# A hybrid retention / linear attention / window attention block: another place and order for the moving sums at both entries of the block products, and an earlier second weight pair

## The chip, the cores and the metric

The kernel runs on one core of one Trainium2 chip. The metric is device time in microseconds of one launch, the median of three runs. A core has TensorE (PE in the profile; PEld are its weight loads), VectorE (DVE), ScalarE (ACT), GpSimd (POOL) and SyncE (SP), which here only issues loads.

## The reference

One transformer block in fp32 on 1024 tokens of width 1024. What the change touches are two sets of large products: the input projection `h @ w_in`, and gate and up of the feed-forward part.

```python
h = rmsnorm(x, norm_mix_pre[l])
proj = h @ w_in[l]                      # q, k, gates of three branches, ...
...
x = x + rmsnorm(merged @ w_out[l], norm_mix_post[l])
h = rmsnorm(x, norm_ffn_pre[l])
f = (jax.nn.silu(h @ ffn_w_gate[l]) * (h @ ffn_w_up[l])) @ ffn_w_down[l]
x = x + rmsnorm(f, norm_ffn_post[l])
```

## The kernel before, in words

Each fp32 operand is kept as two halves, a rounded copy `hi` and the residual `lo`. `split` makes them: ScalarE casts `hi` (L127), then VectorE subtracts to get `lo` (L128; both lines are a helper's). A product of two such operands is three matmuls of 128x128 by 128x512 (L409, L410, L411): hi by hi, hi by lo, lo by hi.

The class `Pairs` (L362) computes two blocks of 128 output features (a *pair*, for instance one block of gate and one of up) over all 1024 tokens. It is a Winograd form of Strassen's scheme: the stationary side are the pair's weights, cut into a11, a12 (first raw tile), a21, a22 (second raw tile); the moving side are the activations, cut into four blocks B11, B12, B21, B22 by feature half and token half. Seven block products replace eight. Each block product is 12 matmuls for one pair:

- `p1` = a11 by b11 into bank x, copied out by `snap` (L359, tile sn); `p2` = a12 by b21 into bank y; the output x copy + y is made by `out` (L1255, L1256: VectorE addition, then Silu on ScalarE);
- `p6` = s2 by t2, on top of x; `p5` = s1 by t1 into bank z; `p7` = s3 by t3 on top of x; `p4` = a22 by t4 on top of x; `p3` = s4 by b22 on top of z.

The weight sums s1 to s4 of a pair are made by `sums` (L384, L386, L388, L389) and `split`; the weights a11 and a12 are split by `blocks` (L379: one cast of 128x1024 into wh and one residual into wl). The moving sums are made once for all pairs, by the class `Sums`: t3 = B22 - B12 (L560), t2 = t3 + B11 (L561), t1 = B22 - t2 (L573, written over t2), t4 = B21 - t2 (L572, in place). Each has four tiles (k = 0 to 3), and each tile is split into a pair of halves.

In the steady state of `steps` a pair's seven products follow one another and everything else runs beside them. At the *entry* the moving sums don't exist yet, so `lead` pairs are taken together: two at the first entry (input projection, `inp`, activations `hf`, from about 82 us), three at the second (`up`, activations `h2f`, from about 1524 us). The entry does all p1 and p2 first, holds back the additions of p2 (`held`), then s2 by t2 for all the lead pairs, then s1 by t1, s3 by t3, then p1 of the next pair (`nxt`), then a22 by t4, p2 of `nxt`, s4 by b22.

The second entry overlaps the end of the output projection. There, a loop over token tiles t (L1276) runs `out_mm(t)` on TensorE and `out_norm(t)` on ScalarE, VectorE and GpSimd; one to three turns later `out_transpose(t)` brings the token tile into `h2f`. The sums t2, t3 need `h2f` of all eight token tiles. `up.fetch` issues weight loads on SP's queue; `up.blocks` and `up.sums` split them.

The order of instructions in each engine's queue is written at build time by Tile's scheduler, which goes by the order in the source, by an estimate of when operands are ready, and by when a slot of a tile pool comes free. Two calls bind it: `keep_in_program_order` (the `Ordered` wrappers, on in part of the first entry) and `issue_after(ins)`, which puts the instructions of a block behind `ins` on its engine. On the chip each queue then runs in that order. The pools are `d` (45 tiles of 128x1024 fp32, or a hi/lo pair of 128x512), `b` (18 tiles of 128x512) and eight banks of PSUM.

Of the kernel before, what the change touches and what calls it, by code (L numbers as in the profile page):

```python
# [12 lines left out]
ALU = mybir.AluOpType  # L13
# [7 lines left out]
NK = D // P  # L21
# [58 lines left out]
def block_kernel(ctx: ExitStack, tc: tile.TileContext, x, vecs, rows, alpha2, w_in, w_branch,  # L80
                 w_out, w_gate, w_up, w_down, cst_in, out):
    nc = tc.nc
    pe, ve, se, po = (Ordered(tc, e) for e in (nc.tensor, nc.vector, nc.scalar, nc.gpsimd))
# [15 lines left out]
    def bt(n, dt=F32):  # L99
        return bp.tile([P, TH], dt, name=f"{n}_{nid()}", tag="b")  # L100
# [4 lines left out]
    def dt_(n, dt=F32):  # L105
        return dp.tile([P, 1024], dt, name=f"{n}_{nid()}", tag="d")

    def bpair(n):
        t = dt_(n, F32R)
        return t[:, :TH], t[:, TH:]  # L110
# [3 lines left out]
    def bank(n):  # L114
        return psp.tile([P, TH], F32, name=f"{n}_{nid()}", tag="ps")
# [10 lines left out]
    def split(hi, lo, src, eng=None):  # L126
        se.copy(out=hi, in_=src)  # L127
        return (eng or ve).tensor_tensor(out=lo, in0=src, in1=hi, op=ALU.subtract)  # L128
# [212 lines left out]
    KH = NK // 2  # L341
# [10 lines left out]
    def moving(name, src):  # L352
        pr = bpair(name)
        split(*pr, src)
        return pr

    def snap(ps):
        c = bt("sn")
        se.copy(out=c, in_=ps)  # L359
        return c  # L360

    class Pairs:  # L362
# [87 lines left out]
        def steps(self):  # L450
            keys, lead = self.keys, self.lead
            first = keys[:lead]
            x, z = self.x, self.z
            self.fetch(lead)
            held = []
            for i, n in enumerate(first):
                if n not in self.ops:
                    self.blocks(n)
                self.p1(n)
                yield  # L460
                held.append(self.p2(n, True))
                yield
            for n in first:
                if "s2" not in self.ops[n]:
                    self.sums(n)
            self.make("t2")
            self.products(first, [x[n] for n in first], "s2", "t2", False)
            for h in held:
                with tc.issue_after(self.sums_of.last.ins):
                    h()  # L470
            for n in first:
                self.sn[n].append(snap(x[n]))
            yield
            self.fetch(lead + 1)
            self.make("t1")
            for n in first:
                self.split(n, "s1")
                z[n] = bank("z")
            self.products(first, [z[n] for n in first], "s1", "t1", True)
            yield  # L480
            self.products(first, [x[n] for n in first], "s3", "t3", False)
            self.make("t4")
            for n in first:
                self.split(n, "a22")
                self.out(n, 1, 1, z[n], snap(x[n]))
            yield
            nxt = keys[lead] if lead < len(keys) else None
            if nxt is not None:
                self.blocks(nxt)
                self.p1(nxt)  # L490
                yield
            self.products(first, [x[n] for n in first], "a22", "t4", False)
            for n in first:
                self.split(n, "s4")
                self.out(n, 1, 0, x.pop(n), None)
            yield
            self.fetch(lead + 2)
            if nxt is not None:
                self.p2(nxt)
                self.sums(nxt)  # L500
                self.split(nxt, "s1")
                yield
            self.products(first, [z[n] for n in first], "s4", "b22", False)
            for n in first:
                self.out(n, 0, 1, z.pop(n), self.sn.pop(n).pop())
                del self.raw[n], self.ops[n]
            yield
            if lead < len(keys):
                self.split(keys[lead], "a22")
                self.split(keys[lead], "s4")  # L510
            for i in range(lead, len(keys)):
                n, nxt = keys[i], keys[i + 1] if i + 1 < len(keys) else None
                self.fetch(i + 3)
                self.p6(n)
                yield
                if nxt is not None:
                    self.blocks(nxt)
                self.p5(n)
                yield
                if nxt is not None:  # L520
                    self.sums(nxt)
                self.p7(n)
                yield
                if nxt is not None:
                    self.p1(nxt)
                    self.split(nxt, "s1")
                    yield
                self.p4(n)
                yield
                if nxt is not None:  # L530
                    self.p2(nxt)
                    self.split(nxt, "a22")
                    yield
                self.p3(n)
                if nxt is not None:
                    self.split(nxt, "s4")
                yield

    def load_pair(w0, c0, w1, c1):
        r = raw_tile(), raw_tile()  # L540
        for raw, wmat, c in zip(r, (w0, w1), (c0, c1)):
            sp.dma_start(out=raw.rearrange("p (k c) -> p k c", k=NK),
                         in_=wmat[:, c:c + P].rearrange("(k p) c -> p k c", p=P))
        return r

    class Sums:
# [21 lines left out]
        def t1(self):  # L568
            res = []
            for k, (t3, t2) in enumerate(self.t):  # L570
                b21, b22 = self.h[k + KH]
                ve.tensor_tensor(out=b21, in0=b21, in1=t2, op=ALU.subtract)  # L572
                ve.tensor_tensor(out=t2, in0=b22, in1=t2, op=ALU.subtract)  # L573
                res.append(moving("t1", t2))
            return res

        def t3(self):
            return [moving("t3", t3) for t3, _ in self.t]

        def all(self):  # L580
            return {"t2": self.t2, "t1": self.t1, "t3": self.t3, "t4": self.block(range(KH, NK), 0)}


    gate_in, gates_gla = {}, []
# [146 lines left out]
    swa_values(2)  # L731
    inp.blocks(ikeys[1])
    next(steps)
    next(steps)
    swa_values(4)
# [137 lines left out]
    def lin_load(i):  # L873

        br, h = divmod(i, H)
        qf, kf = dt_("qf"), dt_("kf")
        sp.dma_start(out=qf, in_=qkd[br][h][0])
        sp.dma_start(out=kf, in_=qkd[br][h][1])
        st = {"q": halves(qf), "k": halves(kf), "v": []}
        for j in range(NT // 2):  # L880
            v2 = dt_("v", F32R)
            sp.dma_start(out=v2.bitcast(F32), in_=vd[i][j])
            st["v"] += [(v2[:, e * DV:(e + 1) * DV], v2[:, TH + e * DV:TH + (e + 1) * DV]) for e in range(2)]
        return st
# [267 lines left out]
    for i in range(2 * H):  # L1152
        br, h = divmod(i, H)
        state["s"] = lin_scores(br, state)
        if i + 1 < 2 * H:
# [6 lines left out]
            nxt = lin_load(i + 1)  # L1162
# [31 lines left out]
    def out_mm(ts):  # L1194

        pss = [[bank("pr"), bank("pr")] for _ in ts]
        for k in range(NK):
            for ps, t in zip(pss, ts):
                lh, ll = (z[:, (t % 4) * P:(t % 4 + 1) * P] for z in ms_[k][t // 4])
                for p_, (rh, rl) in zip(ps, wo[k]):  # L1200
                    pe.matmul(p_, lhsT=lh, rhs=rh, start=(k == 0), stop=False)  # L1201
                    pe.matmul(p_, lhsT=lh, rhs=rl, start=False, stop=False)  # L1202
                for p_, (rh, rl) in zip(ps, wo[k]):
                    pe.matmul(p_, lhsT=ll, rhs=rh, start=False, stop=(k == NK - 1))  # L1204
        return pss
# [62 lines left out]
    up = Pairs(mv, list(range(NF)), lambda f: load_pair(w_gate, f * P, w_up, f * P), up_out, 3, usums)  # L1268
# [7 lines left out]
    for t in range(2, NT):  # L1276
        ps, = out_mm((t,))
        if t == 3:
            out_transpose(0, xns.pop(0))
            out_transpose(1, xns.pop(1))  # L1280
        if t == 4:
            out_transpose(2, xns.pop(2))
        if t == 5:
            up.fetch(1)
            out_transpose(3, xns.pop(3))
            up.make("b11")
            up.make("b21")
        if t == 6:
            up.blocks(0)
            up.fetch(2)  # L1290
            out_transpose(4, xns.pop(4))
        if t == 7:
            up.sums(0)
            out_transpose(5, xns.pop(5))
        xns[t] = out_norm(t, ps, po if t < NT - 1 else ve)
    up.blocks(1)
    next(ups)
    out_transpose(6, xns.pop(6))
    next(ups)
# [30 lines left out]
    pss, nxt = {}, [down_load(*z) for z in [(blocks[0][0], f) for f in blocks[0][1]]]  # L1330
    for bi, (tp, fs) in enumerate(blocks):
        cur = nxt
        if bi + 1 < len(blocks):
            nxt = [down_load(blocks[bi + 1][0], f) for f in blocks[bi + 1][1]]
        first, last = fs[0] == 0, fs[-1] == NF - 1
        for j in range(4):
# [13 lines left out]
            o = [bt("o"), bt("o")]  # L1350
# [40 lines left out]
```

## Time and profile before

| | us |
|---|---|
| median of three runs (lowest, highest) | 2230.72 (2230.05, 2232.22) |
| profiled execution | 2227.39 |
| its span, first to last instruction | 2225.6 |
| TensorE matmul busy in the span | 2118.2 (95%) |
| VectorE busy | 1202.5 (54%) |
| ScalarE busy | 917.1 (41%) |
| GpSimd busy | 241.0 (11%) |

The profile's time and the median of the runs are two measurements of the same program; the profiled execution is 3.33 us below the median. A matmul's end is modelled in the profile, so that busy time of two matmuls in a row overlaps. The granted clock is TensorE's, as a share of 2.4 GHz: 1.00 is 2.4 GHz and 0.50 is 1.2 GHz.

### The profile page before, as it was taken

The numbers are of one execution on the slowest core, as the hardware profiler recorded it, in microseconds if no ns is written. First come the engines' busy times: TensorE is split into PE (matmuls) and PEld (weight loads), VectorE is DVE, ScalarE is ACT, GpSimd is POOL, SyncE is SP. The second block draws the span as 40 slices with busy tenths as digits, with TensorE's granted clock in tenths as the row PEclk, the third lists the DMA queues.
The fourth block names the chain that finished last, engine by engine and source line by source line (L and its number), as shares of the span: only waits on it lengthen the run. The fifth ranks groups of instructions, "written<-read, shape, count | busy, mean of one in ns | idle before, by whom it ended". The sixth has DMA issues, their size and how long they took to land. (4 is left out here: it accounts for less than half of the span.)

```text
span 2225.6 us, 28749 instructions
## 1 busy us (share of the span) xinstructions
PE 2118.2 (95%) x10660; PEld 1792.9 (81%) x10660; DVE 1202.5 (54%) x2215; ACT 917.1 (41%) x1776; POOL 241.0 (11%) x413
## 2 busy tenths in 40 slices
PE   5688999999999999999989999998899999999998
PEld 5567788888889999999967888877688888878786
DVE  3666754444427986655554344426565555544351
ACT  5345444444437775444333212145433333333140
POOL 3011000000012222333321000031000000000000
PEclk9898999999999999999999999999999999999999
DMA  5277655555575446766564535332365555464451
GB/s 184 68 218 224 204 172 161 163 163 166 169 221 173 145 148 210 259 218 204 190 255 156 160 110 156 104 122 87 89 171 142 139 140 142 127 239 164 152 189 38
DMA packets 343277, 364.06 MB, mean 164 GB/s; under 512 B 16464, under 2 KB 267728, under 8 KB 343136
## 3 DMA queue, kind: packets, MB, share of 16 engines
q1 hardware_dynamic: 299776, 265.20, 39.6%
q10 hardware_dynamic: 30816, 54.02, 6.6%
q0 software_dynamic: 12544, 43.00, 5.0%
q8 instruction: 84, 1.38, 0.3%
q14 instruction: 57, 0.47, 0.1%
HBM read 264.64 MB, written 97.52 MB: 163 GB/s over the span
## 5 line engine op out<-in xcount | busy, mean ns | idle before, releaser
L128 DVE TENSOR_TENSOR wl<-raw,wh 128x1024 fp32r<-128x1024 f32 x131 | 160.1, 1223 | 158.2 <-ACT wh L127 80.8
L127 ACT CAST s<-raw 128x512 fp32r<-128x512 f32 x202 | 122.5, 620 | 243.1 <-DVE raw L384 79.8
L127 ACT CAST wh<-raw 128x1024 fp32r<-128x1024 f32 x141 | 147.3, 1047 | 155.0 <-DMA raw<-in_w_down 55.2
L409 PE MATMUL x<-t,s 128*128 128x512 f32 x408 | 161.7, 401 | 21.4 <-ACT sn L359 12.6
L410 PE MATMUL x<-t,s 128*128 128x512 f32 x408 | 163.1, 400 | 0.9 <-DVE t L128 0.7
L411 PE MATMUL x<-t,s 128*128 128x512 f32 x408 | 162.3, 398 | 0.0
L242 PE MATMUL pf<-o,wh 128*128 128x512 f32 x384 | 148.1, 393 | 8.4 <-ACT o L127 8.4
L243 PE MATMUL pf<-o,wh 128*128 128x512 f32 x384 | 149.7, 392 | 0.2 <-DVE o L128 0.2
L359 ACT COPY sn<-x 128x512 f32<-128x512 f32 x151 | 88.4, 586 | 144.5 <-PE x L411 134.9
L257 PE MATMUL v<-wh,hT 128*128 128x256 f32 x512 | 146.4, 286 | 0.0
L259 PE MATMUL v<-wh,hT 128*128 128x256 f32 x512 | 145.4, 284 | 0.0
L258 PE MATMUL v<-wl,hT 128*128 128x256 f32 x512 | 145.4, 284 | 0.0
L1322 PE MATMUL dn<-wh,f 128*128 128x512 f32 x352 | 137.0, 392 | 3.7 <-ACT f L127 3.7
L128 DVE TENSOR_TENSOR s<-raw,s 128x512 fp32r<-128x512 f32 x202 | 136.2, 688 | 2.1 <-ACT s L127 1.5
L1323 PE MATMUL dn<-wl,f 128*128 128x512 f32 x352 | 137.1, 391 | 0.0
L245 PE MATMUL pf<-o,wl 128*128 128x512 f32 x384 | 121.1, 390 | 0.0
L1191 POOL TENSOR_TENSOR rr<-rr,mhalf 128x1 f32<-128x1 f32 x16 | 8.7, 541 | 959.4 <-DVE rr L1190 959.4
L409 PEld LDWEIGHTS x<-t,s 128*128 128x128 f32 x408 | 78.7, 194 | 40.7 <-ACT sn L359 14.3
L1325 PE MATMUL dn<-wh,f 128*128 128x512 f32 x352 | 109.1, 390 | 0.0
L257 PEld LDWEIGHTS v<-wh,hT 128*128 128x128 f32 x512 | 98.7, 193 | 1.2
L258 PEld LDWEIGHTS v<-wl,hT 128*128 128x128 f32 x512 | 98.8, 193 | 1.1
L259 PEld LDWEIGHTS v<-wh,hT 128*128 128x128 f32 x512 | 98.7, 193 | 0.1
(303 smaller groups left out, 5365.8 us busy)
## 6 DMA issues: line engine op xcount, KB each, us to landing
raw<-in_w_in SPq DMA_DIRECT2D x138, 512.0 KB, 6.1
raw<-in_w_down SPq DMA_DIRECT2D x44, 512.0 KB, 6.8
raw<-in_w_gate SPq DMA_DIRECT2D x43, 512.0 KB, 4.8
raw<-in_w_up SPq DMA_DIRECT2D x43, 512.0 KB, 4.7
v<-v POOLq DMA_DIRECT2D x32, 512.0 KB, 4.0
v<-v SPq DMA_DIRECT2D x32, 512.0 KB, 6.5
gT<-go ACTq DMA_DIRECT2D x48, 256.0 KB, 3.9
raw<-in_w_branch SPq DMA_DIRECT2D x24, 512.0 KB, 6.0
```

Of the source, the lines that this page charges most:

```text
L127: se.copy(out=hi, in_=src)
L128: return (eng or ve).tensor_tensor(out=lo, in0=src, in1=hi, op=ALU.subtract)
L242: pe.matmul(p_, lhsT=wh, rhs=hi, start=(k == 0), stop=False)
L243: pe.matmul(p_, lhsT=wh, rhs=lo, start=False, stop=False)
L257: pe.matmul(ps, lhsT=lh, rhs=rh, start=start, stop=False)
L258: pe.matmul(ps, lhsT=lh, rhs=rl, start=False, stop=False)
L259: pe.matmul(ps, lhsT=ll, rhs=rh, start=False, stop=stop)
L409: pe.matmul(ps, lhsT=h, rhs=hi, start=(start and k == 0), stop=False, skip_group_check=True)
L410: pe.matmul(ps, lhsT=h, rhs=lo, start=False, stop=False, skip_group_check=True)
L411: pe.matmul(ps, lhsT=l, rhs=hi, start=False, stop=(k == KH - 1), skip_group_check=True)
L1322: pe.matmul(ps[ch], lhsT=fh[:, ts_], rhs=ws[ch][0], start=(first and i == 0), stop=False)
L1323: pe.matmul(ps[ch], lhsT=fh[:, ts_], rhs=ws[ch][1], start=False, stop=False)
```

## The change

In `Sums`, t1 is now written into the place of block B12 (which is dead once t3 is made), so that t2 stays whole; t4's subtraction moves out of t1 into a function of its own and is made when t4 is asked for. `last`, the instruction behind which the held additions are queued, is now the last residual of t1, not of t2.

In `steps`, t1 is made and the s1 of the lead pairs are split ahead of the held additions and of the copies of x. At the second entry (`lead` = 3) the addition of the first pair is not held any more. The sums of `nxt` are made after its p1, ahead of a22 by t4, no more after its p2.

In the output loop, the second pair's two raw tiles are fetched in turn 5 instead of turn 6, and its `blocks` is made in turn 7, ahead of the first pair's sums, instead of after the loop.

```diff
@@ steps
-                held.append(self.p2(n, True))
+                h = self.p2(n, i or lead < 3)
+                if h:
+                    held.append(h)
                 yield
             for n in first:
                 if "s2" not in self.ops[n]:
                     self.sums(n)
             self.make("t2")
             self.products(first, [x[n] for n in first], "s2", "t2", False)
+            self.make("t1")
+            for n in first:
+                self.split(n, "s1")
             for h in held:
                 with tc.issue_after(self.sums_of.last.ins):
                     h()
...
             self.fetch(lead + 1)
-            self.make("t1")
             for n in first:
-                self.split(n, "s1")
                 z[n] = bank("z")
             self.products(first, [z[n] for n in first], "s1", "t1", True)
...
                 self.p1(nxt)
+                self.sums(nxt)
                 yield
             self.products(first, [x[n] for n in first], "a22", "t4", False)
...
                 self.p2(nxt)
-                self.sums(nxt)
                 self.split(nxt, "s1")
@@ Sums
         def t1(self):
             res = []
             for k, (t3, t2) in enumerate(self.t):
-                b21, b22 = self.h[k + KH]
-                ve.tensor_tensor(out=b21, in0=b21, in1=t2, op=ALU.subtract)
-                ve.tensor_tensor(out=t2, in0=b22, in1=t2, op=ALU.subtract)
-                res.append(moving("t1", t2))
+                o = self.h[k][1]
+                ve.tensor_tensor(out=o, in0=self.h[k + KH][1], in1=t2, op=ALU.subtract)
+                pr = bpair("t1")
+                self.last = split(*pr, o)
+                res.append(pr)
+            return res
+
+        def t4(self):
+            res = []
+            for k, (t3, t2) in enumerate(self.t):
+                o = self.h[k + KH][0]
+                ve.tensor_tensor(out=o, in0=o, in1=t2, op=ALU.subtract)
+                res.append(moving("t4", o))
             return res
...
-            return {"t2": self.t2, "t1": self.t1, "t3": self.t3, "t4": self.block(range(KH, NK), 0)}
+            return {"t2": self.t2, "t1": self.t1, "t3": self.t3, "t4": self.t4}
@@ output loop
         if t == 5:
-            up.fetch(1)
+            up.fetch(2)
             out_transpose(3, xns.pop(3))
             up.make("b11")
             up.make("b21")
         if t == 6:
             up.blocks(0)
-            up.fetch(2)
             out_transpose(4, xns.pop(4))
         if t == 7:
+            up.blocks(1)
             up.sums(0)
             out_transpose(5, xns.pop(5))
         xns[t] = out_norm(t, ps, po if t < NT - 1 else ve)
-    up.blocks(1)
     next(ups)
```

## Rows read from the trace of the kernel before

**Rows 1.** The page's first part, TensorE's line: busy us, share of the span, instructions.

```profile
PE 2118.2 (95%) x10660; PEld 1792.9 (81%) x10660; DVE 1202.5 (54%) x2215; ACT 917.1 (41%) x1776; POOL 241.0 (11%) x413
```

**Rows 2.** Waits of TensorE, first entry then second: waiter <- releaser: us, times, longest.

```profile
PE x L409 <- ACT t L127: 5.6, 1, 5.6
PE z L409 <- ACT s L127: 4.9, 1, 4.9
...
PE z L409 <- ACT s L127: 6.3, 1, 6.3
PE x L409 <- ACT wh L127: 4.0, 1, 4.0
PE x L409 <- ACT s L127: 2.8, 1, 2.8
```

**Rows 3.** Windows: stretch, length, busy PE, PEld, DVE, ACT, POOL, PEclk, DMA share, GB/s.

```profile
88.00:97.00 9.00, 8.58 (x24) 5.67 (x23) 9.00 (x16) 1.99 (x4) 0.00 (x0) 0.67 0.00 0
97.00:102.00 5.00, 0.25 (x2) 0.00 (x0) 4.74 (x9) 4.60 (x10) 1.09 (x2) 0.87 0.60 210
102.00:107.50 5.50, 5.01 (x11) 3.52 (x12) 5.50 (x10) 5.28 (x11) 0.00 (x0) 0.50 0.01 3
...
1531.50:1541.50 10.00, 5.28 (x12) 3.68 (x13) 6.19 (x8) 3.93 (x7) 0.78 (x2) 0.66 0.13 53
...
1551.00:1561.40 10.40, 9.69 (x36) 6.37 (x36) 10.40 (x19) 2.91 (x6) 0.00 (x0) 1.00 0.00 0
...
1567.60:1571.80 4.20, 4.16 (x9) 2.99 (x10) 4.20 (x8) 4.20 (x9) 0.00 (x0) 0.50 0.00 0
1571.80:1599.70 27.90, 27.90 (x124) 22.90 (x122) 13.29 (x21) 8.45 (x15) 0.00 (x0) 1.00 0.21 64
1599.70:1606.00 6.30, 3.54 (x9) 2.67 (x9) 5.99 (x10) 4.37 (x8) 0.00 (x0) 0.73 0.73 203
```

**Rows 4.** Timeline of ScalarE, second entry: start, us, instruction, idle before and releaser.

```profile
1533.37 1.06 ACT L1219 ACTIVATE xn<-x 128x1024 f32<-128x1024 f32 x1 [1.58 <-DVE x L1215]
...
1534.42 1.98 ACT L127 CAST wh<-raw 128x1024 fp32r<-128x1024 f32 x2
...
1561.08 1.28 ACT L1256 ACT_TABLE_LOAD   x1
...
1566.97 1.66 ACT L127 CAST s<-raw 128x512 fp32r<-128x512 f32 x3
...
1598.59 0.62 ACT L127 CAST s<-raw 128x512 fp32r<-128x512 f32 x1 [8.43 <-DVE fo L1264]
```

**Rows 5.** Timeline of VectorE, second entry, same columns.

```profile
1535.50 0.75 DVE L1221 TENSOR_SCALAR xn<-x,rstd 128x1024 f32<-128x1024 f32 x1 [2.82 <-POOL rstd L141]
1536.17 1.22 DVE L128 TENSOR_TENSOR wl<-raw,wh 128x1024 fp32r<-128x1024 f32 x1
...
1542.61 1.13 DVE L1238 TENSOR_SCALAR h2f<-h2t,vec 128x128 f32<-128x128 f32 x4 [2.03 <-PE h2t L1233]
...
1548.60 0.68 DVE L560 TENSOR_TENSOR t<-h2f,h2f 128x512 f32<-128x512 f32 x1
...
1562.67 0.69 DVE L573 TENSOR_TENSOR t<-h2f,t 128x512 f32<-128x512 f32 x1
```

**Rows 6.** Timeline of VectorE, first entry: the first t3 tile.

```profile
84.95 0.69 DVE L560 TENSOR_TENSOR t<-hf,hf 128x512 f32<-128x512 f32 x1
```

**Rows 7.** Groups by line, ScalarE: busy us, mean ns of one, idle before.

```profile
L1256 ACT ACT_TABLE_LOAD x1 | 1.3, 1283 | 0.0
```

**Rows 8.** Timelines of SP's queue and GpSimd, end of the output loop.

```profile
1475.26 0.80 SPq L1209 DMA_DIRECT2D raw<-in_x  x1
1492.23 0.37 SPq L542 DMA_DIRECT2D raw<-in_w_gate  x1
...
1497.92 0.37 SPq L542 DMA_DIRECT2D raw<-in_w_up  x1
...
1510.28 2.53 POOL L1215 TENSOR_TENSOR x<-x,raw 128x512 f32<-128x512 f32 x2 [0.86 <-DVE x L1214]
```

## The prediction, made before the changed kernel ran

> **What bounds the kernel now.** I read the page's first part, then TensorE's waits, then both entries in windows and by timeline. TensorE is busy 95% of the span and no other engine passes 54% [rows 1], so away from the entries time falls only where TensorE has less to do, and this change removes no matmul. What can be won is TensorE's idle time, and the list of its waits [rows 2] shows five at the entries: 5.6 and 4.9 us at the first, 4.0, 6.3 and 2.8 us at the second, 23.6 us together. Behind most of them matmuls also run slowly. At the full granted clock the window from 1571.8 holds 124 matmuls in 27.9 us, 0.225 us each; where the granted clock is 0.50 (1.2 GHz) the window from 1567.6 holds 9 in 4.2 us, 0.46 each, and that from 102.0 holds 11 in 5.5 us [rows 3]. So a wait also costs about 0.2 us for each of the 9 to 12 matmuls behind it. At the entries VectorE is full: 9.00 of 9.00 us, then 10.40 of 10.40 [rows 3]. It is the engine to count against.
>
> VectorE's price per instruction of 128x512: from its L560 at 1548.60 to its L573 at 1562.67 it starts 24 instructions [rows 5], so 14.07 us hold 23 steps of 0.61 us.
>
> **Part 1, the second pair's weights earlier.** Now TensorE waits 4.0 us for the cast wh [rows 2], which stands behind the squares of the last token tile in ScalarE's queue: squares at 1533.37, casts of the second and third pair at 1534.42 [rows 4]. TensorE then does 12 matmuls in the 10 us from 1531.5, at a mean clock of 0.66 [rows 3]. With the cast in turn 7 they can start at 1531.5; four products of 12 (p1, p2 of two pairs) take 48 x 0.225 = 10.8 us, and s2 by t2 could start about 1543 instead of 1551.2 by TensorE alone.
>
> But t2 must exist, and VectorE decides that. Its path now: xn of the last token tile at 1535.50, then the second pair's wl (1.22 us) and weight sums, an idle 2.03 us before the last h2f pieces at 1542.61 (they waited for TensorE's transposes, which stood behind the slow p1), then L560 at 1548.60 [rows 5]. After the change wl is ahead of xn (-1.2 us) and the transposes come before 1541.5 (-2.0): L560 starts 3.2 us sooner. Bound above: the idle 2.82 us before xn [rows 5] also fills with the second pair's sums, 6.0 us. Bound below: the earlier wl and the first pair's early addition and Silu stand in front of the last tile's chain and delay it by up to 1.1 us (wl's 1.22 less its overlap): 2.1 us. I take **3.2 us**, the two rows that must move.
>
> The early fetch puts two loads in front of token tile 5's x on SP's queue. That load issued at 1475.26, the second pair's at 1492.23 and 1497.92 [rows 8]; exchanged, x issues at about 1498 and GpSimd wants it at 1510.28 [rows 8], so 12 us cover a transfer of about 5 us (estimate, the spacing 1492.23 to 1497.92 of two loads). I cost it at nothing. Without that cover the last token tiles come later by what it misses.
>
> **Part 2, t1 and s1 ahead of the held additions.** Now s2 by t2 runs in the window from 1551.0, TensorE then stands 6.3 us until a cast of s1, and its next 9 matmuls run at clock 0.50 [rows 2, 3]. ScalarE spends that time on the table load at 1561.08, three Silus, copies and t1's casts; s1 comes at 1566.97 [rows 4]. From the first t2 matmul (1551.2) to z at 1567.6 are 16.4 us, and 9 x 0.235 = 2.1 us of slow matmuls follow: 18.5.
>
> After the change VectorE has to do, from L560 on, 12 instructions for t2, 8 for t1 and 3 residuals of s1, 23 x 0.61 = 14.0 us; the first t2 matmul comes 2.6 us behind L560 (1548.60 to 1551.2), so z may start 11.4 us behind it. TensorE's own 36 matmuls take 8.1 us and don't hinder. Gain at best 18.5 - 11.4 = 7.1 us. Bound below: a short wait stays and z restarts at the slow clock (-2.1), and t1's residuals between t2's steps add about 1 us: 4.0. I take **6.0 us**, since the casts no longer stand behind Silu and the copies.
>
> The pieces moved: t4's four subtractions now come later, 4 x 0.61 = 2.4 us of VectorE; they hide under s1 by t1 (36 matmuls, 8.1 us) and s3 by t3 (again 8.1); uncovered they cost 2.4. The copies of x, now behind t1 and s1 on ScalarE, have z's 8.1 us before s3 by t3 needs them. Three x, two y and three z are eight banks, so without the first pair's hold z needn't wait for an addition; that I count inside the 6.0.
>
> The first pair's Silu moves from 1562 to about 1533, with the table load of 1.28 us [rows 4] in front of the last token tile's squares. ScalarE sat idle 1.58 us before those squares [rows 4], which covers the load: nothing. There is a single load in Silu's line, with squares and copies all through what follows it [rows 7]. The Trainium skill (ScalarE: Activation LUTs, What ACT_TABLE_LOAD costs, with Table sets: the hidden batching unit) says to batch functions by table set and prices a switch at 2.66 us, load and drain: by it, an early Silu between squares speaks against the change, and the sum would be 1.4 us less gain, or 5.3 us less if the squares needed their own set again. This trace shows 1.28 us and the next instruction right behind it, so the sum leaves the drain out.
>
> **Part 3, the sums of the next pair earlier.** TensorE waits 2.8 us at 1599.7 for s2 of the fourth pair and does 9 matmuls in 6.3 us [rows 2, 3], against 2.0 at the full clock: 4.2 us. The cast of s3, the first link, sat behind 8.43 us of ScalarE's idle time that ended with an L1264 of another pair [rows 4]: the queue held it, not the data. All 4.2 come back if s3 and s2 are done under a22 by t4; nothing if a slot of the pool is what held it, or if the b22 casts are next to be late. I take **2.5 us**, over half, as the cast's place in the queue is what the source moves.
>
> **Part 4, the first entry.** t3 starts at 84.95 [rows 6] and the 5.6 us wait ahead of it stays, as nothing before it moves. VectorE then has 12 + 8 + 2 residuals of s1 + 1 of s2 = 23 x 0.61 = 14.0 us to z, so z may start at 99.0. Now it starts at about 102.0, after 5 us with 0.25 us of matmuls, and runs 5.5 us at clock 0.50, where 11 matmuls lose 2.5 us [rows 3]. Gain between 0.7 (s2 by t2, whose clock is 0.67 now, stretched by the residuals in between) and 3.0 + 2.5 = 5.5. I take **3.8 us**.
>
> **The sum.** 3.2 + 6.0 + 2.5 + 3.8 = 15.5 us, bounds 2.1 + 4.0 + 0 + 0.7 = 6.8 and 6.0 + 7.1 + 4.2 + 5.5 = 22.8. The profiled execution's 2227.4 becomes 2211.9; it lay 3.3 under the median, so 2230.7 becomes **2215**, its own range 2208 to 2224. Behind both entries TensorE is full again, so the gain should carry to the end.
>
> **The rivals.** *VectorE paces both entries.* Each tile of t2 gets two more instructions between its own (t1's difference and residual, where now one difference stands), 4 x 0.61 = 2.4 us for each entry, and the waits shrink to a slow z. Parts 2 and 4 give 2 us in place of 9.8: 15.5 - 7.8 = 7.7, 2223. For it: VectorE is full in both windows [rows 3]. Against: its later work, t3, t4 and b22, has TensorE's two long products as cover.
>
> *The lines move and the instructions don't.* The scheduler writes the queues; if the second pair's cast still lands behind the squares because no two slots are free, and t1's four pairs find none either, parts 1 and 2 fall away and half of 3 and 4 stays: 3.1 us at most, 2228. For it: raw weights lay ready long before 1534 [rows 8] and weren't cast. Against: in the source the cast did stand behind the squares.
>
> *Slower, by the clock.* With t1 in between, matmuls of s2 by t2 come thinner than now, and where they came thinnest (24 in 9 us, first entry) the granted clock was 0.67, at 36 in 10.4 us it was 1.00 [rows 3]. If it falls to 1.2 GHz and stays there through s1 by t1 and s3 by t3 at both entries, 108 + 72 matmuls lose 0.2 each, 36 us, less about 7 that slow ones lose now: 2215 + 29 = 2244. It decides from some 80 more slow matmuls on (15.5 / 0.2). Against: z follows with fewer pauses. The Trainium skill (TensorE: Matmul & The Clock Gate, What's actually happening) has the engine throttled unless it is kept busy, which the 0.50 windows behind the waits agree with.
>
> **How the numbers follow.** Forecast 0.62, VectorE's pace 0.18, nothing moved 0.12, slower by the clock 0.08. 0.2% is 4.5 us, about what a measurement here can tell: the first two are faster, 0.80, the third is the same, the fourth slower. The range 2206 to 2227 runs from under the forecast's best to the edge of the third case and leaves out 0.2: most of the third, the fourth, little below.
>
> **What would show it.** Right: no 4.0 us wait for wh; p1 of the second pair straight behind p2 of the first; L560 of the second entry about 3 us sooner against the output loop's end; waits for s1 before z below 1.5 us at both entries with a clock near 1.00 behind them; the table load before 1540; s3 of the fourth pair cast before the L1264 of the first three. Wrong: a new wait of s2 by t2 over 5 us, a late x of token tile 5, b22 as the new releaser at 1600, or clocks of 0.5 where 1.00 stood.

## The result, and the profile after

The changed kernel takes 2215.12 us (median of 4 runs, 2213.58 to 2215.51); the kernel before, in the same rounds, 2230.39 (2229.32 to 2232.22). The ratio is 0.9929, 95% interval 0.9912 to 0.9947: 15.3 us faster, where 2215 was forecast. The profiled execution took 2215.51 us with a span of 2213.7. That is 11.9 under the span of before, whose profiled execution lay 3 us under its median; sums over traces are made against 11.9.

The page's first part, of the changed kernel:

```profile
PE 2114.9 (96%) x10660; PEld 1790.7 (81%) x10660; DVE 1201.5 (54%) x2215; ACT 916.4 (41%) x1776; POOL 240.6 (11%) x413
```

The same work stands on every engine as in [rows 1]. TensorE's waits at the first entry and then at the second, of the changed kernel:

```profile
PE x L409 <- ACT t L127: 5.6, 1, 5.6
PE x L410 <- DVE t L128: 1.5, 3, 0.7
PE z L411 <- DVE s L128: 0.3, 1, 0.3
PE z L409 <- ACT s L127: 0.3, 1, 0.3
...
PE h2t L1245 <- DVE xn L1233: 3.6, 1, 3.6
PE x L409 <- ACT t L127: 3.3, 1, 3.3
```

Of the five waits of [rows 2], the one for t2 at the first entry stays, as forecast. Those for s1 (4.9 and 6.3 us) and for s2 of the fourth pair (2.8) are gone. The 4.0 us for the second pair's cast are gone too, but in their place stand 3.6 at the last token tile's transposes and 3.3 for t2.

Windows of the changed kernel, columns as in [rows 3]: s2 by t2 and the beginning of z at the first entry, the same two at the second, and the place of the former 2.8 us wait:

```profile
88.36:98.25 9.89, 8.77 (x25) 5.21 (x25) 9.89 (x17) 4.52 (x9) 0.00 (x0) 0.79 0.00 0
98.25:104.05 5.80, 5.50 (x23) 4.11 (x24) 5.80 (x11) 4.12 (x8) 0.55 (x1) 1.00 0.22 80
...
1551.10:1562.07 10.97, 10.97 (x37) 8.62 (x38) 10.97 (x20) 5.54 (x11) 0.00 (x0) 0.74 0.00 0
1562.07:1567.07 5.00, 5.00 (x24) 4.14 (x23) 5.00 (x9) 4.61 (x9) 0.00 (x0) 1.00 0.00 0
1592.07:1602.07 10.00, 10.00 (x46) 8.18 (x45) 5.85 (x10) 3.39 (x7) 0.00 (x0) 1.00 1.03 265
```

z now starts at full clock at both entries. s2 by t2 of the second entry lasts 10.97 us at a clock of 0.74; VectorE, which makes t2, t1 and the residuals, is full in this window too.

To place the gain I use three marks: the first product of the second entry (the first matmul on the gate and up weights, x<-b,wh), L560 behind it (L563 after the change), and the first matmul of z. Before, that first product starts at 1524.83, after at 1523.57. The table shows the distances, from the timelines (us).

| | span start to first product | to t3's first difference (L560, L563) | to z | first product to span end |
|---|---|---|---|---|
| before | 1524.83 | 23.77 | 42.81 | 700.8 |
| after | 1523.57 | 24.94 | 38.50 | 690.1 |

So 10.6 us of the 11.9 are won behind the first product and 1.3 ahead of it. The next two views show what became of the second pair's early weights. VectorE of the changed kernel, second entry, start and duration first:

```profile
1535.69 0.75 DVE L1233 TENSOR_SCALAR xn<-x,rstd 128x1024 f32<-128x1024 f32 x1 [2.61 <-POOL rstd L141]
...
1538.50 1.13 DVE L1250 TENSOR_SCALAR h2f<-h2t,vec 128x128 f32<-128x128 f32 x4 [1.46 <-PE h2t L1245]
1541.70 1.23 DVE L128 TENSOR_TENSOR wl<-raw,wh 128x1024 fp32r<-128x1024 f32 x1 [2.07 <-ACT wh L127]
...
1548.51 0.68 DVE L563 TENSOR_TENSOR t<-h2f,h2f 128x512 f32<-128x512 f32 x1
```

xn of the last token tile came 10.67 us behind the first product before [rows 5], now 12.12. VectorE is idle 2.61, 1.46 and 2.07 us in this stretch and still has weight sums to make before L563. ScalarE of the changed kernel, the same stretch:

```profile
1537.65 0.37 ACT L1252 ACTIVATE h2f<-h2t,vec 128x128 f32<-128x128 f32 x1 [2.47 <-PE h2t L1245]
1538.03 1.28 ACT L1268 ACT_TABLE_LOAD   x1
1539.33 0.63 ACT L1268 ACTIVATE fo<-fo 128x512 f32<-128x512 f32 x1
1539.86 0.87 ACT L1252 ACTIVATE h2f<-h2t,vec 128x128 f32<-128x128 f32 x3
1540.61 1.05 ACT L127 CAST wh<-raw 128x1024 fp32r<-128x1024 f32 x1
```

The table load came 23 us sooner than in [rows 4], and not into the idle time in front of the last tile's squares: it split that tile's four copies, and the third pair's cast waited behind it.

### The profile page after: what moved, and what is told of

The parts are those of the page before. It is cut to its first block, busy times and chain, and to the rows that moved or that the text cites. A ratio compares the mean times of both kernels' runs of the same rounds, so it can differ in the third digit from the quotient of the medians.

```text
span 2213.7 us, 28771 instructions
## 1 busy us (share of the span) xinstructions
PE 2114.9 (96%) x10660; PEld 1790.7 (81%) x10660; DVE 1201.5 (54%) x2215; ACT 916.4 (41%) x1776; POOL 240.6 (11%) x413
## 5 line engine op out<-in xcount | busy, mean ns | idle before, releaser
L127 ACT CAST s<-raw 128x512 fp32r<-128x512 f32 x202 | 122.6, 621 | 242.8 <-DVE raw L384 78.9
L127 ACT CAST wh<-raw 128x1024 fp32r<-128x1024 f32 x141 | 147.4, 1047 | 155.2 <-DMA raw<-in_w_down 58.1
L242 PE MATMUL pf<-o,wh 128*128 128x512 f32 x384 | 148.2, 393 | 8.4 <-ACT o L127 8.4
```

## The experiments

Each kernel ran in five rounds beside the kernel before (2229.61 us in the first four runs' rounds, 2229.79 and 2229.76 in the later ones). "The changed kernel" is the one of the section above. The marks of the table above, for all runs:

| run | median us | ratio to before, 95% interval | to first product | to L563 | to z | first product to end |
|---|---|---|---|---|---|---|
| e1_no_early_weights | 2214.60 | 0.9931 (0.9919, 0.9943) | 1523.16 | 24.56 | 37.16 | 690.0 |
| e2_early_weights_alone | 2228.77 | 0.9996 (0.9988, 1.0005) | 1529.66 | 22.87 | 42.31 | 701.3 |
| e3_next_sums_late | 2218.61 | 0.9944 (0.9931, 0.9956) | 1520.42 | 24.97 | 38.54 | 696.4 |
| e4_first_pair_held | 2213.03 | 0.9925 (0.9912, 0.9938) | 1522.90 | 23.05 | 36.10 | 689.2 |
| e5_first_entry_old_order | 2224.61 | 0.9970 (0.9958, 0.9982) | 1532.90 | 24.88 | 38.60 | 689.8 |
| e6_alpha_on_pool_queue | 2214.72 | 0.9930 (0.9917, 0.9944) | 1525.46 | 24.96 | 38.61 | 690.2 |
| e7_table_early | 2215.32 | 0.9930 (0.9918, 0.9943) | 1524.01 | 24.98 | 38.57 | 689.5 |
| e8_third_weights | 2215.10 | 0.9934 (0.9922, 0.9947) | 1522.63 | 25.39 | 38.74 | 690.6 |
| e9_next_sums_second_entry | 2210.06 | 0.9915 (0.9900, 0.9930) | 1518.41 | 24.94 | 38.48 | 689.9 |
| e11_both_sums_early | 2214.25 | 0.9931 (0.9917, 0.9945) | 1524.99 | 23.93 | 36.53 | 687.7 |
| e12_combined | 2208.76 | 0.9907 (0.9891, 0.9923) | 1519.00 | 22.18 | 35.26 | 687.3 |

The first column of marks is less certain than the others. The kernels e1, e4, e7 and e8 share the changed kernel's first entry and lie, with it, within 1.4 us of each other; e2 shares that of before and lies 4.8 us later in its one trace, while its median agrees with before. Part of this spread has one place: from the first matmul of the output projection (tile pr) to the first product of the second entry, nine of the thirteen traces take 95.0 to 95.1 us, and e2, e5, e6 and e11 take 96.5 to 96.7, at a lower granted clock (shown at e5).

**The second pair's weights** (Part 1), taken out of the changed kernel:

```
-            up.fetch(2)              # turn 5
+            up.fetch(1)
...
+            up.fetch(2)              # turn 6
...
-            up.blocks(1)             # turn 7
...
+    up.blocks(1)                     # behind the loop
```

> The changed kernel without part 1 (second pair fetched and split where the kernel before did it). Theory A, read off the trace after: part 1 removed the wait for wh and gave it back ahead of the t2 sums, so this run is within 2 us of the changed kernel, 2213 to 2217, and L563 of the second entry comes no later against the start of the first p1 than the 24.9 us of the changed kernel. Theory B, the prediction's term: 3.2 us slower than the changed kernel, about 2218.

Measured: 2214.60 us, not told apart from the changed kernel, and 690.0 us behind the first product in place of 690.1. The wait for wh is back with 3.8 us, those of 3.6 and 3.3 are gone or shrunk to 1.4. And that part alone, in the kernel before:

> The kernel before with part 1 alone. Theory A: within 2 us of before, 2229 to 2232, because the t2 sums are not earlier. Theory B: 3.2 us faster than before, about 2227. Theory C, that the early Silu of the first pair (which is not in this kernel) is what ate part 1 in the changed kernel: L560 comes about 2 to 3 us sooner against the first p1 than the 23.8 us of before, and the time falls by as much.

Measured: 2228.77 us, ratio 0.9996 (0.9988, 1.0005), so 2.7 us at the most, less than Theory B's 3.2. Theory C holds in part: without the early Silu, L560 comes 0.9 us sooner behind the first product (22.87 against 23.77), not 2 to 3, and z 0.5 sooner, but the distance from the first product to the end is not shorter (701.3 against 700.8). Part 1 is worth nothing that was measured in either kernel: it exchanges a wait for a wait.

**The next pair's sums late again** (Part 3 undone, at both entries):

```
                 self.p1(nxt)
-                self.sums(nxt)
                 yield
...
                 self.p2(nxt)
+                self.sums(nxt)
```

> The changed kernel with the sums of the next pair back behind its p2 (part 3 undone, both entries). Theory A: about 4.3 us slower than the changed kernel, 2219.5, with the wait of s2 before the fourth pair's p6 back at about 2.8 us and slow matmuls behind it. Theory B: 2.5 us slower, 2217.5. Rival: if a pool slot held the cast of s3, and not its place in the source, no difference.

Measured: 2218.61 us, 3.5 us slower by the medians, with intervals that overlap. The marks split this into two opposite sums: 6.3 us more behind the first product (696.4 against 690.1), and 3.2 less ahead of it. Windows of this run at the fourth pair:

```profile
1588.96:1593.96 5.00, 2.19 (x6) 0.73 0.84 218
1593.96:1598.96 5.00, 5.00 (x15) 0.59 0.67 187
```

Here the columns are stretch, length, TensorE's busy time, clock, DMA share, GB/s. Between them these 10 us hold 21 matmuls; the changed kernel's window at this place (1592.07, above) holds 46 in 10 us. The 2.8 us wait for s2 is back, and behind it the slow clock. That the first entry gets faster without Part 3 was in no forecast; the runs e5, e6 and e9 follow it up.

**The first pair held too.** The change gives up the hold of the first pair's result; here it is kept:

```
-                h = self.p2(n, i or lead < 3)
+                h = self.p2(n, True)
```

> The changed kernel with the first pair's addition held again at the second entry. Theory A1, banks: three y banks are then kept until the held additions behind the last residual of t1, only two banks are left for z, and s1 by t1 starts 2 us or more later: 2217 to 2219. Theory A2, table: the early Silu with its table load sits in the last token tile's copies and costs about 2 us, so holding it makes the t2 sums 2 us earlier: 2212 to 2214. Both at once would cancel to about 2215.

Measured: 2213.03 us; the interval overlaps the changed kernel's, so the difference of 2 us is not shown by the medians. The trace shows where it would come from. ScalarE, then VectorE of this run:

```profile
1561.48 1.28 ACT L1268 ACT_TABLE_LOAD   x1
```

```profile
1545.95 0.69 DVE L563 TENSOR_TENSOR t<-h2f,h2f 128x512 f32<-128x512 f32 x1
```

With the table load back behind s1, L563 comes 23.05 us behind the first product in place of 24.94, and z starts straight behind s2 by t2. So the early addition and Silu, with the table load, cost 1.9 us at L563 (what each of them costs was not separated), and z did not need the bank that the early addition frees.

**The table load moved by itself**, with a Silu of one column on a constant ahead of the last turn:

```
+            warm = sm("warm", 1)
+            se.activation(out=warm, in_=mhalf[:, 0:1], func=AF.Silu)
```

> The changed kernel with one more Silu over a single column, on a constant, ahead of the last token tiles, so that ScalarE's table is loaded before the last token tile's four copies and not between them. If the load of 1.28 us between the copies is what made the third pair's cast and the sums late, L563 starts 1.3 us sooner against the entry's first product and the time falls by 1 to 2 us, to about 2213 to 2214. Rival: the xn of the last token tile, which comes 1.4 us later than before because wl and sums of the second pair stand ahead of it on VectorE, sets the wait of 3.6 us at the transposes whatever ScalarE does: no change beyond 0.5 us.

Measured: 2215.32 us, L563 at 24.98. It decides nothing: the small Silu went to the front of ScalarE's queue (61 instructions in the first 80 us in place of 60), and the table load in the entry stayed between the copies.

**The third pair's weights sooner too:**

```
     next(ups)
+    up.blocks(2)
     next(ups)
```

> The changed kernel with the third pair's weights cast one step sooner as well, ahead of the last token tile's copies. If VectorE's wait of 2.07 us for ScalarE's cast of the third pair is on the path to t2, the wait goes, L563 starts about 2 us sooner and the time is about 2213. Rival: ScalarE has no free time there, so the cast only pushes back the copies of the last token tile and with them x of that tile: L563 does not move, and the time stays within 0.5 us of 2215 or rises by up to 1.5 us.

Measured: 2215.10 us. wl of the third pair waits 1.30 us in place of 2.07, a new wait of 0.85 for a cast of s stands behind it, and L563 comes 0.45 us later. As its rival expected, the cast only changed places with the copies.

**The first entry in the old order**, the second with all of the change:

```
-            self.make("t1")
-            for n in first:
-                self.split(n, "s1")
+            if lead == 3:
+                self.make("t1")
+                for n in first:
+                    self.split(n, "s1")
...
+            if lead != 3:
+                self.make("t1")
             for n in first:
+                if lead != 3:
+                    self.split(n, "s1")
                 z[n] = bank("z")
...
+    mv.update(t1=hsums.t1_old, t4=hsums.block(range(KH, NK), 0))
```

> The changed kernel with the old order at the first entry alone (t1 made from t2 in place and s1 cast only after the held additions); the second entry keeps all of the change. Theory 1, the prediction's Part 4: the first entry's gain reaches the end, so the time goes up by the term of 3.8 us, to about 2219. Theory 2: the gain of 5 to 6 us at the copy of x behind s3 times t3 is there in the changed kernel, but the gate's matmul waits 4.4 us in place of 1.1 for alpha, whose load lands at its own time, so that only about 1.3 us reached the second entry: the time is about 2216.5, and the wait for g is back at about 1 us.

Measured: 2224.61 us, 9.5 over the changed kernel, with ratios whose intervals do not meet. Theory 2 falls, and theory 1 holds in kind but not in size: the gain at the first entry does reach the end, and it is larger than the term. Behind the first product this run is the changed kernel (689.8 against 690.1). Ahead of it: the copy's follower, a22 by t4, starts 6.3 us later, the gate's matmul 6.15 later (152.10 against 145.95), the next wait for a norm 6.4 later (171.40 against 165.02). And the gate's matmul waits 4.2 us here too, so that wait has nothing to do with t1. Some 3 us more come between 170 and the second entry in this trace. Nearly all of them are the clock, at two places: behind a wait of 8.4 us for o (L127) at the same work in both kernels, and at the end of the output loop. This run first, then the changed kernel at the same work:

```profile
1156.89:1162.89 6.00, 5.79 (x17) 4.41 (x18) 3.15 (x6) 3.58 (x7) 0.55 (x1) 0.50 0.72 235
...
1484.24:1492.24 8.00, 7.64 (x27) 6.20 (x28) 2.13 (x5) 4.01 (x13) 3.84 (x5) 0.79 0.70 206
```

```profile
1150.23:1156.23 6.00, 5.78 (x23) 4.28 (x24) 3.35 (x6) 3.58 (x7) 0.64 (x1) 0.68 0.94 321
...
1476.47:1484.47 8.00, 7.65 (x33) 6.30 (x34) 2.11 (x5) 3.99 (x13) 3.86 (x5) 1.00 0.59 177
```

The stretch that holds the first place, from the first matmul on tile pf (L242) to the output projection's first, takes 1.4 us more than in the changed kernel, and the one from there to the second entry 1.6 more. Without these 3.0 us the old order costs 6.2 us in the trace. This run's times go from 2216.97 to 2225.75, so not all 9.5 us belong to the order.

**Alpha's load off SP's queue.** In the changed kernel the gate's matmul waits 4.4 us for alpha, whose load stands on SP's queue behind eight loads of weights (PE, then ScalarE):

```profile
145.95 0.76 PE L631 MATMUL z<-g,a 96*128 96x512 f32 x1 [4.39 <-DVE g L618]
```

```profile
143.61 0.62 ACT L606 CAST a<-al 16x512 fp32r<-16x512 f32 x1 [5.25 <-DMA al<-in_alpha]
```

```
-        sp.dma_start(out=al[:RANK, :], in_=alpha2)
+        po.dma_start(out=al[:RANK, :], in_=alpha2)
```

> The changed kernel with the one load of alpha issued on POOL's queue in place of SP's, where it stands behind eight weight loads that wait for their tiles. If the alpha load swallowed the first entry's gain: the gate matmul's wait of 4.4 us falls to 0 to 1, and the time falls by 3 to 4 us, to about 2211 to 2212. Rival: the waits that follow (4.6 us for the next norm's sum at about 165 us) take up what the gate matmul gives back, and the time stays within 1 us of 2215.

Measured: 2214.72 us, as its rival expected. The gate's matmul starts at 142.78, 3.2 us sooner, and its wait is gone. But waits for the norm take its place. TensorE of this run:

```profile
139.52 0.80 PE L409 MATMUL x<-t,a22h 128*128 128x512 f32 x1 [3.02 <-ACT sn L359]
...
162.94 0.79 PE L409 MATMUL x<-t,s 128*128 128x512 f32 x1 [5.02 <-ACT sn L359]
```

By 669.36, where TensorE next waits for a DMA (of sq), the lead is gone (669.67 in the changed kernel). Alpha is where the delay shows, not what causes it.

**The next pair's sums early at the second entry alone:**

```
                 self.p1(nxt)
-                self.sums(nxt)
+                if lead == 3:
+                    self.sums(nxt)
...
                 self.p2(nxt)
+                if lead != 3:
+                    self.sums(nxt)
```

> The changed kernel with the next pair's sums made early at the second entry alone; at the first entry they stand in their old place. Theory 1, from the run with the sums late at both entries: at the first entry the early sums cost 3 us (there the gate's matmul waited 0.7 us for alpha in place of 4.4, and every later mark up to the second entry lay 3.0 us sooner), at the second they are worth about 6. So the time falls by about 3 us to about 2212, the gate's wait is under 1 us and the wait of 2.8 us for the next pair's sums at the second entry does not come back. Rival: the first entry's 3 us are taken up by a later wait for the norm's sums, as with alpha on POOL's queue, and the time stays within 1 us of 2215.

Measured: 2210.06 us, ratio 0.9915 (0.9900, 0.9930), 5.1 us under the changed kernel's median; the intervals overlap, the marks do not leave it open: the second entry is the changed kernel's (689.9 us behind the first product), and the first product starts 5.2 us sooner, 0.7 of which were there when the first entry began. The gate's matmul of this run:

```profile
142.15 0.47 PE L634 MATMUL z<-g,a 96*128 96x512 f32 x1 [1.33 <-DVE g L621]
```

Why the early sums hurt there is read from the loads and from VectorE. SP's queue from 105 us on, eight loads of weights and then alpha's, start and time from the first issue to the last: the changed kernel, then this run:

```profile
110.45 27.80 SPq L545 DMA_DIRECT2D raw<-in_w_in  x8
138.31 1.66 SPq L603 DMA_DIRECT2D al<-in_alpha  x1
```

```profile
106.27 24.79 SPq L548 DMA_DIRECT2D raw<-in_w_in  x8
134.78 0.39 SPq L606 DMA_DIRECT2D al<-in_alpha  x1
```

VectorE, the residuals of s4, the first pairs' last operand from their raw weights: the changed kernel, where a22 by t4 starts at 111.10, then this run, where it starts at 110.37:

```profile
120.30 1.29 DVE L128 TENSOR_TENSOR s<-raw,s 128x512 fp32r<-128x512 f32 x2 [0.91 <-ACT s L127]
...
122.11 0.68 DVE L128 TENSOR_TENSOR s<-raw,s 128x512 fp32r<-128x512 f32 x1
```

```profile
115.75 0.69 DVE L128 TENSOR_TENSOR s<-raw,s 128x512 fp32r<-128x512 f32 x1
...
117.18 0.68 DVE L128 TENSOR_TENSOR s<-raw,s 128x512 fp32r<-128x512 f32 x1
```

In the changed kernel s4's two are the second of the first row, from about 120.9, and the next row (read from the order of the source; TensorE multiplies with both by 123.3). With the next pair's sums in front of them, these last readers of the first pairs' weights come 9.8 and 11.0 us behind a22 by t4 in place of 5.4 and 6.8. But the first loads were already late before that: the changed kernel's go out at 110.45, when the profile has them wait for TensorE's s3 by t3, and this run's at 106.27, when it has them wait for a residual of VectorE. Alpha, behind them on the queue, is issued 3.5 us later in the changed kernel, 0.7 of which were there when the first entry began. That the sums are the cause is shown by e3 and e9; that it goes by tiles that come free later is read from these rows, not tried by itself, and which tiles these are stays open.

**The first two pairs' sums sooner:**

```
             up.blocks(0)
+            up.sums(0)               # turn 6
...
             up.blocks(1)
-            up.sums(0)               # turn 7
...
+    up.sums(1)                       # behind the loop
     next(ups)
```

> The changed kernel with the weight sums of the first pair one token tile sooner and those of the second pair ahead of the first product, so that on VectorE and ScalarE they no longer stand around the last token tile's norm. Theory 1 for why the second pair's earlier weights brought nothing: VectorE paces t2, the first pair's sums (with casts in front of the last tile's squares on ScalarE) made xn of the last token tile 1.4 us later, and VectorE stood idle 2.6, 1.5 and 2.1 us up to L563 with five sums still to do. Filled, the 3.6 us wait for xn shrinks to about 2, L563 starts 3 to 4 us sooner against the entry's first product, the 3.3 us wait for t2 is gone, and the time falls by 3 us or more, to 2212 or below. Theory 2: the last token tile's own chain (x, its sum of squares, rstd, xn, transposes, copies) sets t2 and the sums only fill its gaps: L563 moves less than 1 us and the time stays within 1 us of 2215.

Measured: 2214.25 us, no difference by the medians. z comes 36.53 us behind the first product in place of 38.50, and 2.4 us are won to the end. The first product comes 1.4 us later in this trace, but not by the sums, which now stand in front of an earlier token tile's norm: from the output projection's first matmul to the first product it takes 96.5 us at the lower clock, and e12, with the same sums, 95.1 like the changed kernel. VectorE of this run:

```profile
1538.11 0.75 DVE L1233 TENSOR_SCALAR xn<-x,rstd 128x1024 f32<-128x1024 f32 x1 [2.62 <-ACT sn L359]
...
1544.22 1.23 DVE L128 TENSOR_TENSOR wl<-raw,wh 128x1024 fp32r<-128x1024 f32 x1 [1.11 <-ACT wh L127]
...
1548.92 0.68 DVE L563 TENSOR_TENSOR t<-h2f,h2f 128x512 f32<-128x512 f32 x1
```

xn comes 1.0 us later, not sooner (13.12 us behind the first product). The idle time in front of it, which ends with rstd in the changed kernel, is 2.5 to 2.8 us in all traces, whatever sums are moved. L563 gains 1.0 us, far from the 3 to 4 of theory 1 and at the edge of theory 2.

**Together:** e9, e11 and the hold of e4.

> The changed kernel with three edits together: the next pair's sums early at the second entry alone, the sums of the first two pairs sooner, and the first pair's result held like the others, so that Silu's table load is not in the last token tile's copies. If the three are independent: about 3 us from the first entry, 3 from the sums, up to 2 from the held pair, so 2207 to 2209. Rival: VectorE paces the second entry whatever is moved, and only the first entry's 3 us come: about 2212.

Measured: 2208.76 us, ratio 0.9907 (0.9891, 0.9923), within the forecast's 2207 to 2209; it has the lowest median of this study, but its interval overlaps those of e9 and of the changed kernel. L563 comes 22.18 us behind the first product, 2.76 sooner than in the changed kernel.

## Why the prediction was right, and where its terms were not

The total was right to 0.1 us, and partly by luck. Of the forecast's 15.5 us the two traces show 11.9 and the medians 15.3; and of the four terms two came 4.4 and 2.5 us short and two 1.8 and 1.5 over. Worked out from the traces, by the marks:

| term | forecast (bounds) | in the trace | how |
|---|---|---|---|
| Part 1 | 3.2 (2.1 to 6.0) | -1.2 | first product to the first t2 matmul, 26.36 before (1551.19), 27.53 after (1551.10) |
| Part 2 | 6.0 (4.0 to 7.1) | 7.8 | first t2 matmul to z, 16.45 before, 10.97 after; and 24 matmuls in z's first 5 us in place of 13, 11 x 0.21 |
| Part 3 | 2.5 (0 to 4.2) | 4.0 | z to the end, 6.3 less, without the 2.3 counted in Part 2 |
| Part 4 | 3.8 (0.7 to 5.5) | 1.3 | span start to first product |

**Part 1 failed as a step**, below its lower bound, and e1 and e2 show no gain from the part in either kernel. The -1.2 of the table holds the early Silu as well: with Part 1 alone the first t2 matmul comes 0.9 us sooner than before (e2: 25.46 us behind the first product), with the early Silu alone 0.8 later (e1: 27.16). What it said of TensorE held: no wait for wh, the second pair's p1 straight behind the first pair's p2 (1530.03). The step that failed is "wl is ahead of xn (-1.2 us) and the transposes come before 1541.5 (-2.0): L560 starts 3.2 us sooner". xn is not paced by VectorE's full queue but by the last token tile's own chain (x, squares, rstd), and what is moved in front of that chain delays it: by 1.45 us here, where 1.1 was the bound (10.67 us behind the first product before, 10.45 in e1, 12.05 in e2). The idle time of VectorE then came back as 1.46 us for the transposes and 2.07 for the third pair's cast. What was costed at nothing for the early fetch held: GpSimd takes token tile 5's x at 1509.00, 14.57 us ahead of the first product, before 14.55 [rows 8].

**"ScalarE sat idle 1.58 us before those squares, which covers the load: nothing" failed too.** Silu is issued when the first pair's addition is done, and that was between the last tile's copies. Held, the addition and Silu give back 1.9 us at L563 (e4). The price itself held: 1.28 us, with Silu starting 1.30 behind the load's start and no drain behind it. The Trainium skill (ScalarE: Activation LUTs, What ACT_TABLE_LOAD costs) gives 1283 ns for the load, which agrees, and about 1380 ns of drain more, which no row here shows; its advice to batch functions by set (Table sets: the hidden batching unit) was right in direction, by the place of the load and not by a second load.

**Part 2 held and was sized low.** The wait for s1 is 0.3 us or none, the clock behind it 1.00, and z came 10.97 us behind the first t2 matmul, where VectorE's pace of 23 steps had given 11.4; the reserve taken off for a short wait and a slow z wasn't needed. Its cost showed in the place that the clock rival named: s2 by t2 itself now runs at 0.74 in place of 1.00. It did not go on into z, so the rival ended there.

**Part 3 is the mechanism that was forecast at the second entry**, where s3 is cast at 1574.13, 24.5 us before the row of before. In the changed kernel it is worth more than the trace of before could show: 6.3 us (e3), since there the 2.8 us wait stands between matmuls at clocks of 0.73 and 0.59. But **the prediction priced the move at the second entry alone**. The same lines run at the first, and there they cost: from the first t2 matmul there to the second entry's first product, 1435.21 us in the changed kernel (1523.57 less 88.36), 1431.11 without the early sums (e3: 1520.42 less 89.31), 1430.79 in e9. That is 4.1 to 4.4 us.

**Part 4 was then sized low and netted away.** From its first t2 matmul to a22 by t4 the first entry took 28.60 us before and takes 22.74 now: 5.9 us, over the upper bound of 5.5, since z starts at 98.25 at full clock. All of it carries to the second entry: before to e3, which has the new order without the early sums, the stretch from the first t2 matmul to the second entry's first product falls from 1437.22 to 1431.11, 6.1 us. With the early sums it falls from 1444.36 (e5), or 1441.4 without the 3.0 us of clock found there, to 1435.21: 6.2 us for the order, and 4.2 for the sums in the old order. What is left in the changed kernel is 6.1 less 4.1, or 2.0, and the first entry began 0.75 us later in this trace: 1.3.

Of the rivals, "VectorE paces both entries" describes the second entry up to z, where nothing that was moved brought L563 more than 2.8 us forward (e12), but not the price it gave to Parts 2 and 4. "The lines move and the instructions don't" and "slower, by the clock" didn't happen.

What stays open: why the clock was lower at two places in four of the thirteen traces, and whether that makes up the 3.4 us between the medians' gain and the traces' (the traces of before and of the changed kernel are both among the other nine).

## What to carry to other kernels

A line moved inside a loop or a shared routine is moved wherever the routine runs: price it at each of its places, and at each ask what it now stands in front of: at the first entry here the weight loads, and alpha's load behind them on the queue, went out some 3 us later. A wait that vanishes is no gain until the next thing late has been named; here casting weights sooner only put them ahead of the chain that set the time. And when a forecast's total is right, check its terms: undoing one move at one place gave 4 to 5 us more than the whole change had, by the traces.

## What the runs showed of the hardware

Behind the same waits of TensorE the granted clock came out differently from trace to trace. Two waits of 1.2 and 1.0 us at the end of the output loop left it at 1.00 in the changed kernel and in eight other traces; in e2, e5, e6 and e11 it was 0.79 over 8 us there (a mean of its two levels, 1.2 and 2.4 GHz), and the stretch took 1.4 to 1.6 us more for the same instructions. The same four traces ran at 0.50 over the 6 us behind the 8.4 us wait for o, where the changed kernel had 0.68, and lost about 1 us more there. What decides it no run here shows. A single trace can't tell such a piece from the effect of an edit further up; the distance between two marks that lie close to the edit can.
